# Loads of the late modulation on GpSimd's queue, with two places of their own beside three for the weights

## The chip, the cores and the metric

The kernel runs on one core of one Trainium2 chip. The metric is device microseconds of that core for one execution. Five engines matter here: TensorE (PE, with its weight loads shown as PEld), VectorE (DVE), ScalarE (ACT), GpSimd (POOL) and SyncE (SP), which does nothing but issue transfers. The times of the kernel before are those of three runs; the profile and its trace are of a further execution.

## The reference, cut to what matters

One layer of a diffusion backbone over 256 latent tokens with 256 context tokens, 2048 channels wide, all in float32. What is computed, cut to the parts that this change touches or lies beside:

```python
sh1, sc1, g1, sh2, sc2, g2 = jnp.split(jax.nn.silu(c) @ w_ada[l] + b_ada[l], 6, axis=-1)
... = split_columns(modulate(rmsnorm(x, norm_mix[l]), sh1, sc1) @ w_in[l])
# latent attention (q, k, v from low-rank projections) and gated DeltaNet, both branches
y_l = merge_branches(y_mla_l, dn_output(o_dn_l, ...), lga, lgb, w_o_mla[l], w_o_dn[l], w_out[l])
x = x + jnp.expand_dims(g1, -2) * y_l
x = x + jnp.expand_dims(g2, -2) * conv_glu(
    modulate(rmsnorm(x, norm_ffn[l]), sh2, sc2), w_ffn_up[l], ffn_conv[l], w_ffn_down[l])
```

The modulation `silu(c) @ w_ada` has six parts of 2048 numbers. The first two (`sh1`, `sc1`) are needed at once. The other four (`g1`, `sh2`, `sc2`, `g2`) are needed late: `g1` behind the output projection, `sh2` and `sc2` ahead of the feed-forward part, `g2` at the very end. These four are "the late modulation"; their weights are 64 MB, read as 128 tiles of 512 KB.

## The kernel before, in words

**Weights.** Nearly all of the time is matrix products of float32 weights with activations. A tile of weights (128 partitions x 1024 columns, 512 KB) is loaded into one of five **places** in SBUF (tag `raw`, `NR = 5`, a ring: the n-th load goes where the (n-5)-th was). ACT casts each half of it (512 columns) to `whi` (line 121), DVE subtracts to get the rest `wlo` (line 122), and PE multiplies by both parts (helper `mm_hl`; all PE instructions carry line 68). There are six places for halves of `whi` and of `wlo` (`NH = 6`). A `raw` place is free again when the `wlo` of its second half is done. `load_w` (line 130) does this for one block of columns, `raw_w` (line 124) issues the load on SP's queue (line 127).

**The late modulation.** `ada_rest` (line 254) is a generator that is run beside everything else: each step takes one of the 128 tiles of `wada2`, and one DVE instruction (line 279, shown as a custom operation) multiplies it with a row `sch` that stands on all partitions and sums it up, in place. `load(i)` (line 257) takes a place of the same ring of five (tag `raw`) and issues the load on SP's queue (line 260). It is called one step ahead: step i asks for tile i+1 and then reduces tile i. `sch` holds one half of the silu'd condition; it is loaded anew when the half changes (line 273, five times, on SP's queue).

**How it is spread.** `Side` (line 234) runs such a generator by debts: `ada(ns)` adds to what is owed, and steps of 1300 ns are taken until nothing is owed. How many steps come at which place of the program is thus fixed. They come in the DeltaNet heads (17 tiles), in the attention (`side`, line 1152 and on, 45), in the scan (line 1362, about 20), in the output projection `wout` (line 1409, 19) and in the feed-forward loop (line 1476, 27). The stages by the time at which they run: heads from 130 us, latent projections from 345, attention from 450, scan from 720, DeltaNet's output projection `wodn` from about 930, `wout` from 985, the change to the feed-forward part from 1075, its loop from 1110, its last product `wdown` from 1550 us to the end. In attention and scan, products for the gates (`gtp`, weights `wz`, `wgm`, `wgd`) and the attention's output projection (`brp`, `womla`) are put between the short, dependent products.

**What sets the order.** Engines run their own queue in order, and an instruction waits for what it reads and for its place. The program's order is not quite the queues' order: the framework plans the queues by its own costs, except for engines in stretches that are pinned (`Ordered`, line 58, keeps those in the program's order; loads by `sync.dma_start` are not pinned, those by `osync` are). On SP's queue lie the weights' loads (line 127), the late modulation's loads (line 260), the scan's small loads (lines 1225 to 1249) and others; an entry whose place is not free yet holds up all behind it. POOL has 50 instructions in the whole kernel: the power -1/2 for the norms (`rsq`, line 173) and a few fills.

**The early loads.** `load_shift` (line 329) loads the weights of `sh1` into the same ring of five.

Of the kernel before, what the change touches and what calls it, by code (L numbers as in the profile page):

```python
# [8 lines left out]
F32 = mybir.dt.float32  # L9
# [7 lines left out]
P = 128  # L17
# [9 lines left out]
G3 = 96 + 256 * N1  # L27
GR = 1024
GH = 512
NR = 5  # L30
NH = 6
AD = 0.55
GD0 = 2
# [20 lines left out]
def hybrid_block(ctx: ExitStack, tc: tile.TileContext, io, dbg=None):  # L54
    nc = tc.nc
    act, dve, pool, sync = nc.scalar, nc.vector, nc.gpsimd, nc.sync
# [23 lines left out]
    def pool_(name, bufs, side="left"):  # L80
        return tc.tile_pool(name=name, bufs=bufs, side=side, reuse_waits="tile")
# [5 lines left out]
    wr = ctx.enter_context(pool_("wr", 2))  # L87
# [31 lines left out]
    def split(raw, hi, lo):  # L119

        act.copy(hi, raw)  # L121
        dve.tensor_tensor(out=lo, in0=raw, in1=hi, op=ALU.subtract)  # L122

    def raw_w(src):
        n = src.shape[1]
        raw = wr.tile([P, GR], F32, tag="raw", name="raw", bufs=NR)[:, :n]
        sync.dma_start(raw, src)
        return raw

    def load_w(src):  # L130

        g = []
        for o in range(0, src.shape[1], GR):
            raw = raw_w(src[:, o : min(o + GR, src.shape[1])])
            for i in range(0, raw.shape[1], GH):
                n = min(GH, raw.shape[1] - i)
                hi = wp.tile([P, GH], F32R, tag="whi", name="whi", bufs=NH)[:, :n]
                lo = wp.tile([P, GH], F32R, tag="wlo", name="wlo", bufs=NH)[:, :n]
                split(raw[:, i : i + n], hi, lo)
                g.append((hi, lo))  # L140
        return lambda o, m=P: tuple(w[:, o % GH : o % GH + m] for w in g[o // GH])
# [12 lines left out]
    def mm_hl(ps, M, w, x, first, last):  # L154

        hi, lo = w
        xf = x.rearrange("p a b -> p (a b)")
        if last and not first:
            pe.matmul(ps[:M, :T], lo, x[:, 0, :], start=False, stop=False)
            pe.matmul(ps[:M, :], hi, xf, start=False, stop=True)  # L160
        else:
            pe.matmul(ps[:M, :], hi, xf, start=first, stop=False)
            pe.matmul(ps[:M, :T], lo, x[:, 0, :], start=False, stop=last)
# [90 lines left out]
    def ada_rest():  # L254


        def load(i):
            w = wr.tile([P, GR], F32, tag="raw", name="rawa", bufs=NR)
            c, n = divmod(i, 32)
            sync.dma_start(w, io["wada2"][c, (n // 16 + c) % 2, n % 16])  # L260
            return w

        parts = ad.tile([P, 2, 16], F32, name="parts")
        half, ahead = None, load(0)
        for i in range(128):
            c, n = divmod(i, 32)
            h, j = (n // 16 + c) % 2, n % 16
            if h != half:

                for _ in range(1 if i else 0):  # L270
                    yield 1300
                half, sch = h, ad.tile([P, GR], F32, tag="sch", name="sch")
                sync.dma_start(sch, Sc[h])
                for _ in range(3):
                    yield 1300
            w = ahead
            if i < 127:
                ahead = load(i + 1)
            dve.tensor_tensor_reduce(out=w, in0=w, in1=sch, scale=1.0, scalar=0.0, op0=ALU.mult, op1=ALU.add, accum_out=parts[:, h, j : j + 1])  # L279
            if n == 31:  # L280
                cs = slice(16 * c, 16 * c + 16)
                dve.tensor_tensor(out=adaT[:, cs], in0=parts[:, 0], in1=parts[:, 1], op=ALU.add)
                dve.tensor_tensor(out=adaT[:, cs], in0=adaT[:, cs], in1=bada[:, 32 + 16 * c : 48 + 16 * c], op=ALU.add)
                ada.done = c + 1
            yield 1300
# [41 lines left out]
    Sc = dram.tile([2, P, GR], F32, name="Sc")  # L327

    def load_shift(p):
        raws = []  # L330
        for m in range(4):
            raws.append(wr.tile([P, GR], F32, tag="raw", name="raw", bufs=NR))
            osync.dma_start(raws[m], io["wadab"][p, m])
        return raws

# [74 lines left out]
    def load(*what):  # L410
        for kind, n in what:
            d, f = {"w": (wts, load_scale), "s": (shifts, load_shift), "g": (grs, load_first)}[kind]
            d[n] = f(n)
# [101 lines left out]
    def gather(ps, M, out, scale=None):  # L515

        act.copy(out, ps[:M, T:])  # L517
        dve.tensor_tensor(out=out, in0=ps[:M, :T], in1=out, op=ALU.add)
# [240 lines left out]
    def head_inputs(h, side=lambda c: None):  # L759
# [12 lines left out]
        gather(ps, P, xq[:, 0])  # L772
        return xs[0], xs[1], xq

    ada = Side(ada_rest())
    ada.done = 0
    ins = {h: head_inputs(h) for h in (3, 0)}
# [191 lines left out]
    def mm3(ps, a, b, first, last):  # L969

        pe.matmul(ps, a[0], b[0], start=first, stop=False)
        pe.matmul(ps, a[0], b[1], start=False, stop=False)
        pe.matmul(ps, a[1], b[0], start=False, stop=last)
# [187 lines left out]
    for b in range(4):  # L1161
        at, pr = mla_attend(b), mla_project(b + 1) if b < 3 else iter(())
        for n in range(7):
            for st in (pr, tail, at):
                c = next(st, None)
# [289 lines left out]
    for f in range(NFF):  # L1455
# [19 lines left out]
        split(y, glu(f)[:, 0], glu(f)[:, 1])  # L1475
        ada(1000)
    ada.finish()
    for f in range(KD):
        ps = psm.tile([P, 512], F32, tag="mm", name="dps")
        W = load_w(io["wdown"][f])  # L1480
        for k in range(NFF):
            if f == KD - 1:
                mm3(ps[:, :T], W(k * P), (glu(k)[:, 0], glu(k)[:, 1]), k == 0, k == NFF - 1)
            else:
                mm_hl(ps, P, W(k * P), glu(k), k == 0, k == NFF - 1)
        yx = pf2.tile([P, T], F32, tag="fy", name="yo")
        src = ps[:, :T]
        if f < KD - 1:
            gather(ps, P, yx)
            src = yx  # L1490
        dve.scalar_tensor_tensor(out=yx, in0=src, scalar=adaT[:, 48 + f : 49 + f], in1=x1[:, f], op0=ALU.mult, op1=ALU.add)
        sync.dma_start(io["out"][f], yx)
# [103 lines left out]
```

## Time and profile before

| | |
|---|---|
| median of 3 runs | 1815.59 us (1812.57 to 1816.42) |
| the profiled execution | 1812.06 us |
| its span in the trace | 1810.3 us |
| PE busy | 1754.9 us, 97% of the span |
| DVE busy | 1366.4 us, 75% |
| ACT busy | 918.4 us, 51% |
| POOL busy | 46.1 us, 3% |
| read from HBM | 388.57 MB |

The page gives busy time by engine, a chain of waits that ended last, and groups of instructions. Other views used below: sums by stretch of time, groups of one stretch, who waited for whom, transfers with the median time from issue to landing, and the timeline. A row of groups reads: line, engine, operation, output<-inputs, shape, count, then busy time and mean duration of one in ns, then idle time of the engine just before and what ended it. In a row of stretches each engine has its busy time and number of instructions, then come PE's granted clock, the busy share of the 16 transfer engines and the rate.

### The profile page before, as it was taken

Reading aid. Unit: us, or ns where it says so; the run is one execution under the profiler, and the core shown is the slowest. Engines: PE = TensorE matmul, PEld = TensorE weight load, DVE = VectorE, ACT = ScalarE, POOL = GpSimd, SP = SyncE. Lnnn points to the kernel's source line nnn. Section 1 sums busy time; section 2 is a strip of 40 time slices with the busy share of each in tenths; the row PEclk is TensorE's granted clock in tenths of the full one; section 3 lists DMA queues with packets and bytes.
Section 4 is the critical chain, followed back from the end, with each engine's and each line's share of the span. In section 5 each row is a group of like instructions: output and inputs, shape, how many; then the busy total and the mean of one; then the engine's idle time right before and its main releaser. Section 6 shows DMA issues by size and latency. Waiting matters only on the chain.

```text
span 1810.3 us, 33551 instructions
## 1 busy us (share of the span) xinstructions
PE 1754.9 (97%) x12701; PEld 1520.6 (84%) x12701; DVE 1366.4 (75%) x2764; ACT 918.4 (51%) x1866; POOL 46.1 (3%) x50
## 2 busy tenths in 40 slices
PE   7999999999989999898999999999999999999999
PEld 6887887887878887787878888888888888888888
DVE  4787899778777787576669989888788888655554
ACT  3344444444666665433346555555555555544443
POOL 0000011000000000000010000000000000000000
PEclk9999999999999999999989999999999999999999
DMA  9973788764778767887766985777667777666663
GB/s 387 414 298 100 214 235 231 221 211 130 230 226 252 230 213 244 304 268 273 259 211 188 317 301 186 253 225 238 189 212 226 224 233 224 184 201 199 198 198 123
DMA packets 195011, 419.76 MB, mean 232 GB/s; under 512 B 61280, under 2 KB 101344, under 8 KB 192416
## 3 DMA queue, kind: packets, MB, share of 16 engines
q1 hardware_dynamic: 167664, 402.37, 68.9%
q10 hardware_dynamic: 27184, 15.23, 2.7%
q8 instruction: 100, 1.64, 0.4%
q14 instruction: 63, 0.52, 0.1%
HBM read 388.57 MB, written 28.84 MB: 231 GB/s over the span
## 4 chain that ended last, share of the span: by engine, by line
PE 75%; issue 9%; DMA 8%; DVE 6%; ACT 2%; POOL 1%; SPq 0%; POOLq 0%; ACTq 0%; DVEq 0%
PE fps L68 25%; PE dps L68 13%; PE mmp L68 11%; PE gtp L68 8%; PE fp L68 4%; DMA rawa<-in_wada 3%; PE brp L68 2%; DVE wlo L122 2%; DMA raw<-in_wadab 1%; PE amp L68 1%; PE vps L68 1%; PE op L68 1%; PE tp L68 1%; DVE rawa L279 1%; PE kps L68 1%
## 5 line engine op out<-in xcount | busy, mean ns | idle before, releaser
L122 DVE TENSOR_TENSOR wlo<-raw,whi 128x512 fp32r<-128x512 f32 (+1 forms) x940 | 632.4, 685 | 202.5 <-ACT whi L121 194.7
L121 ACT CAST whi<-raw 128x512 fp32r<-128x512 f32 (+1 forms) x940 | 573.7, 619 | 404.0 <-PE dps L68 113.7
L68 PE MATMUL fps<-H,whi 128*128 128x512 f32 x1376 | 473.9, 393 | 1.8 <-DVE H L1433 1.7
L68 PE MATMUL fps<-H,wlo 128*128 128x256 f32 x1376 | 371.6, 280 | 0.1
L68 PEld LDWEIGHTS fps<-H,whi 128*128 128x128 f32 x1376 | 253.1, 188 | 53.2 <-issue 1.9
L68 PEld LDWEIGHTS fps<-H,wlo 128*128 128x128 f32 x1376 | 259.2, 188 | 7.6 <-DVE wlo L122 0.5
L68 PE MATMUL gtp<-h,whi 128*128 128x512 f32 x640 | 232.5, 400 | 5.0 <-ACT whi L121 5.0
L68 PE MATMUL mmp<-h,whi 128*128 128x512 f32 x640 | 226.9, 397 | 0.0
L68 PE MATMUL dps<-GB,whi 128*128 128x512 f32 (+1 forms) x595 | 195.7, 378 | 0.0
L279 DVE CUSTOM_DVE_ANT_0 rawa<-rawa,sch 128x1024 f32<-128x1024 f32 x128 | 155.9, 1220 | 38.5 <-DMA rawa<-in_wada 37.7
L68 PE MATMUL gtp<-h,wlo 128*128 128x256 f32 x640 | 175.1, 284 | 5.5 <-DVE wlo L122 5.4
L68 PE MATMUL mmp<-h,wlo 128*128 128x256 f32 x640 | 176.1, 281 | 0.3 <-DVE wlo L122 0.3
L68 PE MATMUL dps<-GB,wlo 128*128 128x256 f32 x560 | 154.1, 280 | 0.0
L68 PEld LDWEIGHTS gtp<-h,whi 128*128 128x128 f32 x640 | 120.7, 190 | 30.1 <-ACT whi L121 6.6
L68 PEld LDWEIGHTS mmp<-h,whi 128*128 128x128 f32 x640 | 119.0, 188 | 24.6 <-issue 0.4
L68 PEld LDWEIGHTS gtp<-h,wlo 128*128 128x128 f32 x640 | 121.6, 190 | 13.3 <-DVE wlo L122 9.1
L68 PEld LDWEIGHTS dps<-GB,whi 128*128 128x128 f32 x595 | 109.2, 188 | 21.2
L68 PEld LDWEIGHTS mmp<-h,wlo 128*128 128x128 f32 x640 | 120.3, 188 | 3.6 <-DVE wlo L122 1.0
L68 PEld LDWEIGHTS dps<-GB,wlo 128*128 128x128 f32 x560 | 105.1, 188 | 0.6
L68 PE MATMUL fp<-h,gh 128*128 128x256 f32 (+1 forms) x448 | 85.3, 291 | 2.7 <-ACT h L68 1.7
L68 PEld LDWEIGHTS fp<-h,gh 128*128 128x128 f32 (+1 forms) x448 | 69.7, 190 | 7.6 <-issue 4.1
L517 ACT COPY fx<-fps 128x256 f32<-128x256 f32 x86 | 31.8, 372 | 65.7 <-PE fps L68 65.7
(565 smaller groups left out, 2553.4 us busy)
## 6 DMA issues: line engine op xcount, KB each, us to landing
rawa<-in_wada SPq DMA_DIRECT2D x128, 512.0 KB, 4.7
raw<-in_wgate SPq DMA_DIRECT2D x82, 512.0 KB, 4.4
raw<-in_wval SPq DMA_DIRECT2D x82, 512.0 KB, 4.5
raw<-in_wdown SPq DMA_DIRECT2D x80, 512.0 KB, 4.2
wt<-in_wadas SPq DMA_DIRECT2D x16, 1024.0 KB, 10.5
raw<-in_wadab SPq DMA_DIRECT2D x32, 512.0 KB, 8.7
raw<-in_wgm SPq DMA_DIRECT2D x32, 512.0 KB, 4.7
raw<-in_wgd SPq DMA_DIRECT2D x32, 512.0 KB, 5.4
```

The lines of the kernel that those rows point to most:

```text
L68: i = f(*a, **k)
L121: act.copy(hi, raw)
L122: dve.tensor_tensor(out=lo, in0=raw, in1=hi, op=ALU.subtract)
L279: dve.tensor_tensor_reduce(out=w, in0=w, in1=sch, scale=1.0, scalar=0.0, op0=ALU.mult, op1=ALU.add, accum_out=parts[:, h, j : j + 1])
L517: act.copy(out, ps[:M, T:])
```

## The change

The ring of five is cut in two while the late modulation runs: three places (tag `raw`) for the weights, two (tag `rawa`) for the late modulation. Its loads and the five loads of `sch` are issued on GpSimd's queue in place of SP's. Ahead of the late modulation (`load_shift`) and behind it (`wdown`), the weights use all five places in turn: `raw_tile` counts and sends two of five loads to the `rawa` places.

```diff
-NR = 5
+NR = 3
+NA = 2
...
+    place = [0, True]
+    def raw_tile():
+        place[0] += 1
+        spare = place[1] and place[0] % (NR + NA) >= NR
+        return wr.tile([P, GR], F32, tag="rawa" if spare else "raw", name="raw", bufs=NA if spare else NR)
...
     def raw_w(src):
         n = src.shape[1]
-        raw = wr.tile([P, GR], F32, tag="raw", name="raw", bufs=NR)[:, :n]
+        raw = raw_tile()[:, :n]
         sync.dma_start(raw, src)
...
         def load(i):
-            w = wr.tile([P, GR], F32, tag="raw", name="rawa", bufs=NR)
+            w = wr.tile([P, GR], F32, tag="rawa", name="rawa", bufs=NA)
             c, n = divmod(i, 32)
-            sync.dma_start(w, io["wada2"][c, (n // 16 + c) % 2, n % 16])
+            pool.dma_start(w, io["wada2"][c, (n // 16 + c) % 2, n % 16])
...
-                sync.dma_start(sch, Sc[h])
+                pool.dma_start(sch, Sc[h])
...
-            raws.append(wr.tile([P, GR], F32, tag="raw", name="raw", bufs=NR))
+            raws.append(raw_tile())
...
+    place[1] = False
     ada = Side(ada_rest())
...
     ada.finish()
+    place[1] = True
     for f in range(KD):
         ps = psm.tile([P, 512], F32, tag="mm", name="dps")
```

## Prediction

> **What bounds the kernel now.** First the page, for the share of each engine:
>
> ```profile
> span 1810.3 us, 33551 instructions
> PE 1754.9 (97%) x12701; PEld 1520.6 (84%) x12701; DVE 1366.4 (75%) x2764; ACT 918.4 (51%) x1866; POOL 46.1 (3%) x50
> ```
>
> PE is busy for 1754.9 of 1810.3 us. Whatever the change does to waits of DVE or SP, it can take from the time only what is PE's idle time now, 55.4 us, and it can add without limit. So the second view asks in which stages PE idles (sums by stretch: length, PE, PEld, DVE, ACT, POOL, clock, busy share of the transfer engines, GB/s):
>
> ```profile
> 130.00:345.00 215.00, 211.75 (x1792) 178.43 (x1791) 180.84 (x393) 103.39 (x215) 15.96 (x14) 1.00 0.68 200
> 345.00:450.00 105.00, 101.21 (x867) 84.72 (x867) 89.20 (x190) 51.57 (x106) 5.02 (x6) 1.00 0.61 176
> 450.00:720.00 270.00, 256.75 (x1911) 224.29 (x1910) 203.56 (x438) 170.59 (x388) 17.53 (x15) 0.97 0.74 231
> 720.00:900.00 180.00, 165.57 (x1361) 142.62 (x1361) 120.51 (x286) 70.36 (x141) 0.00 (x0) 0.99 0.83 279
> 900.00:985.00 85.00, 81.29 (x688) 69.64 (x683) 69.71 (x171) 42.54 (x93) 4.56 (x4) 0.94 0.59 194
> 985.00:1075.00 90.00, 90.00 (x518) 79.09 (x517) 82.53 (x163) 48.18 (x101) 0.00 (x0) 1.00 0.89 309
> 1120.00:1530.00 410.00, 410.00 (x2364) 360.39 (x2363) 335.39 (x650) 227.86 (x444) 0.00 (x0) 1.00 0.72 227
> ```
>
> PE idles 13.2 us in the attention (450 to 720) and 14.4 us in the scan (720 to 900). In the heads, the latent projections and before `wout` it idles 3.3, 3.8 and 3.7 us. In `wout` (985 to 1075) and in the feed-forward loop it never idles: there the change can only lose. The time to be won lies in two stages, 27.7 us at most.
>
> **Attention.** The third view, groups of DVE, transfers and SP's waits of that stretch (a wait's row: us in total, times, longest), then DVE's timeline round PE's longest idle time:
>
> ```profile
> L279 DVE CUSTOM_DVE_ANT_0 rawa<-rawa,sch 128x1024 f32<-128x1024 f32 x45 | 54.9, 1222 | 28.8 <-DMA rawa<-in_wada 28.1 <-DMA sch<-Sc 0.6
> ```
> ```profile
> rawa<-in_wada SPq DMA_DIRECT2D x45, 512.0 KB, 4.7
> ```
> ```profile
> SPq L260 <- DVE wlo L122: 22.0, 16, 3.0
> SPq L260 <- DVE parts L279: 20.6, 11, 4.3
> ```
> ```profile
> 515.53 0.20 DVE L1109 TENSOR_SCALAR mns<-mns,qm 128x1 f32<-128x1 f32 x1
> 518.30 1.23 DVE L279 CUSTOM_DVE_ANT_0 rawa<-rawa,sch 128x1024 f32<-128x1024 f32 x1 [2.57 <-DMA rawa<-in_wada]
> 519.46 0.08 DVE L279 DVE_READ_ACCUMULATOR2_ANT parts<- 128x1 f32 x1
> 519.46 0.16 DVE L1011 SCALAR_TENSOR_TENSOR km<-ks,krm 128x4 f32<-128x4 f32 x1
> ```
> ```profile
> 519.67 0.58 PE L68 MATMUL vps<-whi,kvn 128*128 128x256 f32 x1 [4.04 <-DVE km L1011]
> ```
>
> DVE stands still 28.1 us for tiles of the late modulation, which nobody needs before `wout`, 470 us later. Once this reaches PE: from 515.7 DVE waits for a tile, `km` stands behind it in DVE's queue, and PE idles 4.04 us for `km`. The loads come late because SP issues them late: at line 260 it waits 42.6 us in these two rows, mostly for a place.
>
> *With the change* a load waits only for the place of two steps before. 45 steps in 270 us are one in 6.0 us, so a place has 12.0 us for one turn. What POOL takes for an issue the trace doesn't show. The nearest rows are 0.33 us for SP's issue and 1.12 us for POOL's power:
>
> ```profile
> L260 SPq DMA_DIRECT2D rawa<-in_wada x128: 327/328/652, 170.0 to 1516.7; - x128
> ```
> ```profile
> L173 POOL TENSOR_TENSOR l2m<-l2m,half 128x4 f32<-128x4 f32 (+1 forms) x16 | 18.0, 1124 | 331.0 <-DVE l2m L683 331.0
> ```
>
> [...] A turn is then 1.1 + 4.7 (landing) + 1.3 (reduction with its read) = 7.1 us, under 12.0. Waits are left only where three steps come in one burst. Of the 28.1 us of DVE I expect under 12 to be left; of PE's idle time I count the 4.04 us that are plainly from this and 0.5 us more: **-4.5 us**. Bounds: -13.2 (all of the stage's idle time), +4 (bursts bring the same waits back beside another small operation).
>
> **Scan.** Groups of PE and waits of SP in 720 to 900, then SP's timeline in it:
>
> ```profile
> L68 PE MATMUL gtp<-h,whi 128*128 128x512 f32 x209 | 77.5, 406 | 5.0 <-ACT whi L121 5.0
> L68 PE MATMUL gtp<-h,wlo 128*128 128x256 f32 x210 | 58.4, 289 | 5.5 <-DVE wlo L122 5.4
> L68 PE MATMUL brp<-YM,whi 128*128 128x512 f32 x88 | 32.6, 401 | 1.9 <-ACT whi L121 1.9
> L68 PE MATMUL brp<-YM,wlo 128*128 128x256 f32 x88 | 23.0, 282 | 2.0 <-DVE wlo L122 2.0
> ```
> ```profile
> SPq L260 <- DVE wlo L122: 25.0, 8, 6.8
> SPq L260 <- DVE parts L279: 8.8, 2, 8.5
> ```
> ```profile
> 799.26 0.52 SPq L127 DMA_DIRECT2D raw<-in_wgd  x1
> 808.37 0.33 SPq L260 DMA_DIRECT2D rawa<-in_wada  x1
> 808.79 1.26 SPq L1247 DMA_DIRECT2D jit<-As  x2
> ...
> 813.01 0.33 SPq L127 DMA_DIRECT2D raw<-in_wgd  x1
> 813.84 0.33 SPq L127 DMA_DIRECT2D raw<-in_womla  x1
> ```
>
> All of the stage's idle time is PE waiting for split weights (5.0 + 5.5 + 1.9 + 2.0 = 14.4 us). Ahead of it SP stands 33.8 us in its queue at loads of the late modulation without a place, and the weights' and the scan's loads stand behind them: 8.5 us from 799.8 to 808.4 in the lines shown. On POOL's queue such a wait holds up nothing here, since POOL has no instruction in this stage (0.00 in the row of stretches). Against it stand the three places: weights that were fetched four at a time now come three at a time. 38 loads (26 `wgd`, 12 `womla`) in 180 us through three places leave 14 us for a turn, enough on the mean, not within a bunch. I count 6 of the 14.4 us, under half: **-6 us**. Bounds: -14.4 and +4 (two bunches cut by the third place, at a landing time each).
>
> **`wout`.** This is where three places are tight. Transfers, SP's waits and DVE's main row of 985 to 1075, and the page's row of the casts:
>
> ```profile
> raw<-in_wout SPq DMA_DIRECT2D x30, 512.0 KB, 5.2
> rawa<-in_wada SPq DMA_DIRECT2D x18, 512.0 KB, 5.3
> ```
> ```profile
> SPq L127 <- DVE wlo L122: 17.6, 16, 2.9
> SPq L127 <- DVE parts L279: 17.6, 12, 3.5
> ```
> ```profile
> L122 DVE TENSOR_TENSOR wlo<-raw,whi 128x512 fp32r<-128x512 f32 x66 | 44.0, 685 | 3.3 <-ACT whi L121 3.1
> ```
> ```profile
> L121 ACT CAST whi<-raw 128x512 fp32r<-128x512 f32 (+1 forms) x940 | 573.7, 619 | 404.0 <-PE dps L68 113.7
> ```
>
> About 32 tiles of weights (two small ones among them) and 18 others pass five places in 90 us: 10 turns a place, 9.0 us each, and SP waits 35.2 us for places, so they bind already. Afterwards three places make 32/3 = 10.7 turns: 8.4 us each. The least turn is landing 5.2, two casts and one `wlo` (0.62 + 0.62 + 0.69), 7.1 us; what lies between that and 9.0 is DVE's queue (82.53 of 90 us busy) and waiting. If a turn stays at 9.0 us, the stage grows by 10.7 x 0.6 = 6.4 us; if it gets under 8.4, by nothing. Half of the waits were for `parts`, that is for places held by the other kind, and these go. I take a third of the way: **+2 us**, bounds 0 and +6.4.
>
> **The rest.** In the feed-forward loop 150 tiles pass three places in 410 us, 8.2 us a turn:
>
> ```profile
> raw<-in_wval SPq DMA_DIRECT2D x75, 512.0 KB, 4.5
> ```
> ```profile
> ACT whi L121 <- PE fps L68: 85.2, 142, 1.2
> ```
>
> Landing 4.5 and the same 1.9 make 6.4 us, and the casts there wait for PE (85.2 us, 142 times): tiles land early and the six halves behind are full. So **0**, bound +4 (where a late tile's bytes come in between and ACT's stock doesn't cover it). In the stages 345 to 450 and 900 to 985 no late modulation runs, and two of five places lie idle: **+1**, bounds 0 and +4. POOL's powers (18.0 us for 16, 1124 ns each) stand behind a load's issue now and then: 128 issues of 1.1 us in some 1350 us, a tenth of the time, over 36 powers, half an issue each: 36 x 0.1 x 0.55 = 2 us, of which half is hidden by other products: **+1**, bounds 0 and +4. The wait that is added in POOL's queue is for a reduction two steps back, which stands in DVE's queue ahead of what the next power reads, so it holds up no power by itself. The `sch` loads (five) cost as the others do.
>
> **Sum**: -4.5 - 6 + 2 + 0 + 1 + 1 = -6.5 us. Against the profiled execution's own 1812.06 us (span 1810.3 and 1.8 around it) that is 1805.6. The median of the runs shown, 1815.59, is 3.5 us above it, so against the median the forecast is **1809.1 us**. A measurement of this kernel can tell about 0.2% (3.6 us) from no change.
>
> **Rivals.**
>
> *Three places are too few* (slower). In `wout` a turn stays at 9.0 us (+6.4), PE has no idle time to give there, the stages without late modulation lose their bound (+4), the feed-forward loop starts short (+2), the powers +1, and in the scan the cut bunches eat the gain (0); the attention's -4.5 is kept. +9: 1824.5 us. It decides from a turn of 8.4 us in `wout`. For it: PE at 90.00 of 90 us and the transfers at 0.89 there. Against it: the 17.6 us of waits for `parts`, which go. Chance 0.29.
>
> *The same transfers on another queue* (no change). The bytes and the 16 engines are the same, at 0.83 busy in the scan. If what PE waits for there is bytes and not SP's order, the tiles land no earlier: attention -4.5, scan 0, losses +4: 1815.1 us. Against it: 33.8 us in which SP stood with nothing to do. Chance 0.22. [...]
>
> *POOL's loads are slow* (slower). Over 12.0 - 1.3 = 10.7 us from release to landing, every step in the attention waits: DVE's 28.1 us come back and more, gains there turn into +4, the scan keeps half (-3), losses +4: 1820.6 us. Chance 0.05. [...]
>
> **How the numbers follow.** Forecast 0.44, the others 0.29, 0.22 and 0.05. What no view shows is how the framework plans the queues anew; it moves every case by some us. The likeliest case's own range is 1803 to 1812 (won 12 us to 4 us). The wide range goes from 60% of the 27.7 us won and nothing lost (1815.6 - 16.6 = 1799) to 1828, the first rival with some us more. Faster 0.44, same 0.22, slower 0.34.
>
> **What would show it.** Right: DVE's idle time for `rawa` in the attention under 12 us; PE's in the scan at 8 us or less and no long gap in SP's queue; POOL's issues near 1.1 us; `wout` still with PE near its full time. Wrong: PE idle in `wout` or in the feed-forward loop for `whi` or `wlo`; turns there over 8.4 us; `rawa` landing over 10 us; powers on POOL behind a load.

## The result, and the profile after

| | before | after |
|---|---|---|
| median | 1814.16 us (4 runs, 1812.57 to 1816.42) | 1885.4 us (4 runs, 1876.95 to 1888.6) |
| ratio | | 1.0384, 95% interval 1.0348 to 1.0421 |
| the profiled execution, its span | 1812.06, 1810.3 us | 1884.88, 1883.1 us |

The changed kernel is slower by some 70 us, far outside the range of the prediction. First the changed kernel's page, the same two lines that the prediction starts from:

```profile
span 1883.1 us, 33670 instructions
PE 1776.1 (94%) x12701; PEld 1537.9 (82%) x12701; DVE 1373.1 (73%) x2764; ACT 922.4 (49%) x1866; POOL 116.4 (6%) x183
```

PE has the same 12701 products, is busy 21.2 us longer, and idles 107.0 us where it idled 55.4. To see where, both traces are cut at the same marks: 120 us, the first product of the attention's keys, the first of the scan, the first of the scan's norm, the first of `wout`, the first of the feed-forward part, the first of `wdown`. So the rows are heads with the latent projections, attention, scan, `wodn`, `wout`, feed-forward loop. Columns as in the prediction. The kernel before:

```profile
120.00:443.00 323.00, 318.09 (x2737) 270.00 (x2735) 273.57 (x584) 154.26 (x321) 20.99 (x20) 1.00 0.66 196
443.00:747.90 304.90, 287.89 (x2097) 250.13 (x2096) 225.03 (x474) 189.30 (x423) 17.53 (x15) 0.98 0.75 236
747.90:934.70 186.80, 174.00 (x1525) 150.58 (x1526) 129.71 (x318) 69.80 (x143) 0.00 (x0) 0.99 0.80 269
934.70:993.40 58.70, 54.99 (x401) 46.19 (x401) 53.79 (x132) 33.10 (x76) 4.56 (x4) 0.91 0.54 171
993.40:1087.60 94.20, 90.64 (x565) 80.04 (x563) 84.16 (x164) 49.74 (x102) 0.70 (x1) 1.00 0.88 303
1087.60:1568.00 480.40, 480.22 (x2753) 421.43 (x2754) 393.26 (x769) 269.10 (x527) 0.00 (x0) 1.00 0.70 219
```

The changed kernel, cut at the same marks:

```profile
120.00:471.50 351.50, 329.93 (x2754) 278.98 (x2743) 301.56 (x633) 153.24 (x319) 49.42 (x73) 0.96 0.74 228
471.50:832.90 361.40, 304.10 (x2097) 262.24 (x2096) 267.76 (x563) 191.76 (x426) 58.41 (x94) 0.89 0.79 254
832.90:1000.70 167.80, 167.80 (x1523) 149.29 (x1521) 111.35 (x280) 71.31 (x142) 0.00 (x0) 1.00 0.74 229
1000.70:1057.80 57.10, 53.10 (x401) 44.73 (x401) 51.38 (x127) 31.50 (x74) 4.59 (x4) 0.97 0.55 169
1057.80:1157.30 99.50, 93.17 (x566) 81.78 (x564) 69.18 (x129) 52.98 (x106) 0.69 (x1) 0.97 0.66 196
1157.30:1640.40 483.10, 481.27 (x2752) 421.38 (x2753) 366.13 (x713) 268.76 (x527) 0.00 (x0) 1.00 0.62 187
```

The heads took 28.5 us more and the attention 56.5 us more; the scan took 19.0 us less; the rest makes some 7 us. VectorE's column tells what happened: in the attention it has 563 instructions where it had 474, in the feed-forward loop 713 where it had 769. The late modulation has moved. Its reductions, first the kernel before, then the changed one (ns: least, median, greatest; first and last start in us):

```profile
L279 DVE CUSTOM_DVE_ANT_0 rawa<-rawa,sch x128: 1205/1219/1227, 173.7 to 1521.4; 128x1024 f32<-128x1024 f32 x128
```
```profile
L288 DVE CUSTOM_DVE_ANT_0 rawa<-rawa,sch x128: 1201/1219/1277, 136.9 to 801.9; 128x1024 f32<-128x1024 f32 x128
```

All 128 are now done by 803 us: 49 in the heads (17 before) and 79 in the attention (47). Counted in VectorE's queue, the last of them stood behind 2234 of its 2508 other instructions and now stands behind 1039. The generator still takes its steps where it did; but the reductions and their loads are not pinned, and with places of their own they no longer wait for the weights' turn, and the framework's planner put them far earlier.

The price, in one place. VectorE's timeline of the changed kernel, then PE's:

```profile
494.32 1.22 DVE L288 CUSTOM_DVE_ANT_0 rawa<-rawa,sch 128x1024 f32<-128x1024 f32 x1
...
497.81 1.23 DVE L288 CUSTOM_DVE_ANT_0 rawa<-rawa,sch 128x1024 f32<-128x1024 f32 x1 [2.26 <-DMA rawa<-in_wada]
...
502.52 1.23 DVE L288 CUSTOM_DVE_ANT_0 rawa<-rawa,sch 128x1024 f32<-128x1024 f32 x1 [3.48 <-DMA rawa<-in_wada]
...
505.35 1.23 DVE L288 CUSTOM_DVE_ANT_0 rawa<-rawa,sch 128x1024 f32<-128x1024 f32 x1 [1.59 <-DMA rawa<-in_wada]
...
518.00 1.23 DVE L288 CUSTOM_DVE_ANT_0 rawa<-rawa,sch 128x1024 f32<-128x1024 f32 x1 [1.34 <-DMA rawa<-in_wada]
519.16 0.08 DVE L288 DVE_READ_ACCUMULATOR2_ANT parts<- 128x1 f32 x1
519.16 0.16 DVE L1021 SCALAR_TENSOR_TENSOR km<-ks,krm 128x4 f32<-128x4 f32 x1
```
```profile
519.46 0.60 PE L69 MATMUL ks<-ones,ksq 128*32 128x1 f32 x32 [19.99 <-DVE km L1021]
```

Eight reductions stand in a row; from 494.3 to 519.2 us VectorE does nothing else. Two places hold two loads in flight, so seven of the eight wait for a landing (0.78 to 3.48 us each), and `km` of 0.16 us, the first of the attention's eight, stands behind them all. In the kernel before it was the third `km` that held PE, for 4.04 us behind one load; now the first holds it for 19.99 us behind eight. The group of the attention's reductions, whose idle time was to fall under 12 us:

```profile
L288 DVE CUSTOM_DVE_ANT_0 rawa<-rawa,sch 128x1024 f32<-128x1024 f32 x79 | 96.4, 1221 | 50.7 <-DMA rawa<-in_wada 47.7 <-DMA sch<-Sc 2.9
```

It rose from 28.8 to 50.7 us.

### The profile page after: what moved, and what is told of

The parts are those of the page before. It is cut to its first block, busy times and chain, and to the rows that moved or that the text cites. A ratio compares the mean times of both kernels' runs of the same rounds, so it can differ in the third digit from the quotient of the medians.

```text
span 1883.1 us, 33670 instructions
## 1 busy us (share of the span) xinstructions
PE 1776.1 (94%) x12701; PEld 1537.9 (82%) x12701; DVE 1373.1 (73%) x2764; ACT 922.4 (49%) x1866; POOL 116.4 (6%) x183
## 3 DMA queue, kind: packets, MB, share of 16 engines
q0 software_dynamic: 19152, 69.74, 11.7%
## 4 chain that ended last, share of the span: by engine, by line
PE 60%; issue 22%; DMA 8%; DVE 6%; POOL 3%; ACT 1%; SPq 0%; POOLq 0%; DVEq 0%; ACTq 0%
PE fps L69 25%; PE dps L69 13%; PE mmp L69 5%; PE gtp L69 4%; DMA rawa<-in_wada 3%; PE fp L69 3%; PE brp L69 3%; POOL rawa L269 2%; DVE rawa L288 1%; DMA raw<-in_wadab 1%; DVE wlo L123 1%; PE amp L69 1%; DMA raw<-in_wz 1%; PE op L69 1%; DMA sch<-Sc 1%
## 5 line engine op out<-in xcount | busy, mean ns | idle before, releaser
L123 DVE TENSOR_TENSOR wlo<-raw,whi 128x512 fp32r<-128x512 f32 (+1 forms) x940 | 639.7, 686 | 244.7 <-ACT whi L122 230.1
L69 PE MATMUL gtp<-h,whi 128*128 128x512 f32 x640 | 237.0, 407 | 0.0
L69 PEld LDWEIGHTS dps<-GB,whi 128*128 128x128 f32 x595 | 109.3, 188 | 21.2
L269 POOL DMA_DIRECT2D rawa<-in_wada x128 | 69.3, 542 | 577.9 <-DVE parts L288 369.0
```

Of the source, the lines that this page charges most:

```text
L69: i = f(*a, **k)
L269: pool.dma_start(w, io["wada2"][c, (n // 16 + c) % 2, n % 16])
```

## The experiments

The theories at first. **T1**: the reductions come too early, because nothing holds them. **T2**: GpSimd's queue is at fault. **T3**: three places are too few for the weights. The parts were taken singly (places, queue), and the changed kernel was given an edge (an order between two instructions that the planner has to keep) that holds its reductions in the program's order.

**places_only** and **queue_only**: the diff of the change without its `pool.dma_start`, and nothing but its `pool.dma_start`.

> The changed kernel with the loads on SyncE's queue: places of their own, no new queue, no edge. T1: the planner again hoists the reductions (112 of 128 lie among VectorE's first 1034 others, the last 16 reach to the 1334th), so the time stays near the changed kernel's: 1855 to 1890 us. T2: about 1815 us. T3: 1870 to 1890 us.

> The kernel before with the loads on GpSimd's queue: the ring of five stays shared. T1: the reductions stand as before (last at 2235), so 1805 to 1830 us, whatever the new queue is worth by itself. T2: 1870 to 1890 us. T3: 1805 to 1825 us.

Measured: places_only 1.0121 (1.0090 to 1.0152), queue_only 1.0105 (1.0079 to 1.0131) times the kernel before; medians 1835.29 and 1835.13 us. Each part costs about 1%, both together 3.8%: the parts don't add, and no theory had said that. places_only hoists (moves its reductions forward) nearly as far as the changed kernel (45 reductions in the heads, 67 in attention) and loses a third as much, so T1 in its plain form fell here; it misses queue_only by 5 us too. T2 and T3 miss both kernels by 10 us or more. In queue_only the reductions stand on the mean 4 instructions from where they stood, the last one behind 2234 others as before, so its 1% is not their order.

**held** and **held_sp**: the changed kernel, and places_only, with one edge.

```diff
-            dve.tensor_tensor_reduce(out=w, ...)
+            red = dve.tensor_tensor_reduce(out=w, ...)
+            tc.keep_in_program_order(red)
```

> The changed kernel with one edge more: each of the 128 reductions may not be issued ahead of the vector instruction that the program has before it. Theory T1 (the reductions come too early: with places of their own nothing holds them, so the planner puts them all among the first 1040 of VectorE's 2510 other instructions, where before they reached to the 2235th): the last one goes back to place 2291, heads and attention fall back to about 323 and 305 us from 351.5 and 361.4, and the time lies in the range of the prediction, 1799 to 1828 us, near 1810. Theory T2 (GpSimd's queue is at fault: its loads are slow, or its powers stand behind its loads): it stays at 1870 to 1890 us. Theory T3 (three places are too few for the weights): 1870 to 1890 us as well.

> As held, but the loads of the late modulation come from SyncE's queue again. T1: 1799 to 1828 us, within some 8 us of held. T2: about 1815 us, and 55 us or more below held. T3: 1870 to 1890 us.

Measured: held 1.0091 (1.0070 to 1.0112), 1832.29 us; held_sp 1.0075 (1.0055 to 1.0096), 1829.08 us. The edge alone takes 53 us of the loss back, with GpSimd's queue and three places left as they are, so T2 and T3, which gave held 1870 us or more, fall; both times lie 1 to 4 us above the upper end that T1 gave. The rows of held for heads, attention and `wout`:

```profile
120.00:447.50 327.50, 322.56 (x2766) 273.60 (x2758) 275.96 (x586) 155.26 (x321) 30.99 (x39) 0.99 0.64 191
447.50:760.30 312.80, 288.92 (x2098) 250.72 (x2098) 223.69 (x471) 189.81 (x426) 41.94 (x62) 0.97 0.74 237
991.50:1101.60 110.10, 93.30 (x566) 80.76 (x564) 86.22 (x167) 49.63 (x103) 10.81 (x20) 0.95 0.78 266
```

Heads and attention are back within 8 us each of the kernel before; `wout` is 15.9 us longer. Between held and held_sp, with one order, the medians are 3 us apart and the intervals overlap. By stages the queue does tell: with the loads on GpSimd's queue the scan is 9.8 us shorter (173.7 for 183.5), and attention and `wout` are 4.3 and 6.0 us longer (312.8 for 308.5, 110.1 for 104.1). Their transfers (median us from issue to landing), held first:

```profile
rawa<-in_wada POOLq DMA_DIRECT2D x128, 512.0 KB, 5.3
```
```profile
rawa<-in_wada SPq DMA_DIRECT2D x128, 512.0 KB, 4.5
```

A load from GpSimd lands 0.8 us later in this pair, and 0.2 us later in the pair before_order and before_order_sp below (5.2 and 5.0).

**before_held**: the edge on the kernel before.

> The kernel before (five shared places, SyncE's queue) with the edge of held. It prices the edge by itself: if held and held_sp lost their 14 to 16 us to the edge, this one takes 1825 to 1835 us; if they lost them to the three places and the new queue, 1811 to 1818 us.

Measured: 1.0261 (1.0235 to 1.0287), 1862.19 us, above both expectations. With five shared places the program's own order is dear by itself, which was not foreseen; its row for `wout`:

```profile
1009.10:1135.40 126.30, 103.86 (x566) 84.40 (x564) 87.17 (x165) 50.13 (x102) 1.09 (x1) 0.94 0.70 225
```

At that order, places of their own are worth a good deal: held_sp, with three and two, takes 33 us less than this kernel with five shared. With this T3 is out as the cause of the 70 us.

**unburst**: the changed kernel, with an edge on the reductions 50 to 56, which breaks up the eight of above.

```diff
+            if 50 <= i < 57:
+                tc.add_manual_dep(red.ins, kms[0].ins.name, ...)
```

> The changed kernel with one edge for the reductions 50 to 56: not ahead of the first key statistic km of the attention. It breaks up the one place where the changed kernel has eight reductions in a row on VectorE, with km behind them and TensorE idle for 19.99 us; the first 50 reductions stand where they stood, and no run longer than four is left, that at the very end. Theory W (what costs is the wait: reductions that stand in a row wait for a load each, two at a time, and the small operation behind them holds TensorE): 15 to 25 us less than the changed kernel, 1860 to 1870 us. Theory D (what costs is VectorE's work alone: 128 reductions of 1.2 us in the two stages): 1878 to 1890 us.

Measured: 1.0300 (1.0264 to 1.0336), 1869.42 us: 16 us less than the changed kernel, within what W gave. The trace is less clear: the 19.99 us are gone, the attention is 8.0 us shorter (353.4 for 361.4), and PE now waits 12.7 and 7.2 us at its end for the weights of `brp`. So one burst was worth less than its own length.

**lead32**: the changed kernel, a reduction at most 32 steps ahead of its place.

```diff
+            seen.append(last_dve())
             red = ...
+            if i >= 32:
+                tc.add_manual_dep(red.ins, seen[i - 32], ...)
```

> The changed kernel where a reduction may come at most 32 steps ahead of its place in the program. Heads and latent keep the 48 or so reductions of the changed kernel, attention falls from 79 to about 44, scan to wout get some again, and 16 are left for the feed-forward part. If hoisting is the cause, the time lies between held (1832) and the changed kernel (1885): 1850 to 1865 us, with heads still at about 350 us. If it is the queue or the number of places, 1875 to 1890 us.

Measured: 1.0160 (1.0119 to 1.0200), 1842.91 us, less than expected. Heads 348.8 us with 48 reductions, as said; attention 309.4 us with 47.

**same_order**: the changed kernel, each reduction not ahead of the instruction behind which it stands in places_only.

```diff
+    BEHIND = [1929, 1929, 1697, 1669, ...]
...
+            tc.add_manual_dep(red.ins, "I-%d" % BEHIND[i], ...)
```

> The changed kernel (loads on GpSimd's queue, two places, three for the weights), with an edge for each reduction: not ahead of the vector instruction behind which it stands in places_only. VectorE's order is then nearly that of places_only, which differs from the changed kernel in the loads' queue alone and took 1835 us; no eight reductions stand in a row. If the 50 us between places_only and the changed kernel come from the order that the planner chose for the new queue (the reductions more crowded), it takes 1835 to 1850 us, with heads at 326 to 332 us. If they come from the queue itself (issue and landing of its loads, its powers), 1870 to 1885 us, with heads near 350 us.

Measured: 1.0202 (1.0165 to 1.0240), 1852.48 us, just above the range for the order and well below that for the queue. In the trace the reductions stand on the mean 3 instructions from where they stand in places_only. Of the 50 us between places_only and the changed kernel, some 33 are the order that the planner chose when the loads went to GpSimd. The other 17 are the queue at a crowded order together with what the edges and a new plan of SyncE's queue may add; no run here parts them. The heads, same_order then places_only:

```profile
120.00:456.90 336.90, 328.17 (x2789) 277.41 (x2787) 301.35 (x631) 156.69 (x325) 47.84 (x68) 0.98 0.74 231
```
```profile
120.00:446.20 326.20, 319.00 (x2737) 270.62 (x2736) 296.70 (x626) 153.84 (x321) 20.99 (x20) 1.00 0.77 241
```

**Five attempts at a better kernel, and what they say of number and crowding.** The scan is some 19 us shorter without its reductions (167.7 us in places_only), and places_only had 28 more in the heads for 3.2 us. So the steps were moved: **moved** (the kernel before, three rates changed), **fenced2** and **fenced3** (places_only, the same kind of rates, the reductions that come from `wout` on held behind a fence at its start, and behind a second one at the feed-forward part), **moved_held_sp** (held_sp with the rates of moved), **moved_part** (its edge from attention on only).

```diff
-AD = 0.55
+AD = 0.33
...
-ADS = 0.3
+ADS = 0.0
...
-ADB = 4000
+ADB = 11500
```

The further edits of the fenced kernels (AD 0.5 and 0.53, ADS 0.0, ADB 8000 and 9000) and of moved_part:

```diff
+            if fence[0]:
+                tc.add_manual_dep(red.ins, fence[0], ...)
...
+    behind()
     while ada.done < 1:
```
```diff
+            if hold[0]:
+                tc.keep_in_program_order(red)
...
+    hold[0] = True
     pe.pinned = True
     for c in mla_project(0):
```

> The kernel before with three rates changed and nothing else: 48 of the late modulation's reductions in the stage of the heads (17 before), 29 in attention (48), none in the scan (18), 18 in wout, 33 in the feed-forward part. From the runs so far heads took 28 more for 3.2 us, attention 20 more for 26 us, and the scan without its 18 was 19 us shorter. If a reduction's price is set by the stage where it stands, 1775 to 1800 us. If early reductions are dear wherever they stand, 1825 us or more.

> places_only with two fences: the reductions that the program has from wout on may not come before wout, and those of the feed-forward part not before it; none is traced in the scan. So 45 reductions in the heads, 30 in attention, none in the scan and wodn, 24 or so in wout, the rest behind. If prices by stage add up (heads 3 us over the kernel before, as in places_only; attention 20 us under it, as 18 fewer at 1.1; scan 19 us under it; wout and the feed-forward part 5 us over), 1780 to 1795 us. If early reductions in the heads cost 25 to 29 us, as in moved and lead32, 1805 to 1825 us.

> As fenced2, with rates that bring 80 reductions ahead of the scan: 47 in the heads, 33 in attention, 18 or so in wout. By the prices of the stages within 5 us of fenced2: 1780 to 1797 us; 1805 to 1825 us if the heads cost 25 us more.

> Two places of their own and three for the weights on SyncE's queue, the edge of held, and the rates of moved: 48 reductions in the heads, 29 in attention, none in the scan, 19 in wout, each at its place in the program and so evenly spread. If early reductions are cheap when they are spread and have places of their own (theory W), heads take 326 to 335 us, attention 294 to 302, the scan 168, wout 104 to 110, and the whole 1795 to 1812 us. If their number in the heads or the three places cost (moved: heads 352.4 us with the five shared), heads take 345 us or more and the whole 1820 to 1835 us.

> As moved_held_sp, but the edge only from attention on: in the heads the planner may hoist again. Theory W: hoisting in the heads costs as little as in places_only (326.2 us for 45 reductions), so heads 326 to 333 us and the whole 1793 to 1810 us, within 5 us of moved_held_sp. If the number counts, 1820 to 1835 us as well.

| kernel | reductions: heads, attention, scan, `wout`, after | heads, attention, scan, `wout`, feed-forward us | ratio, 95% interval |
|---|---|---|---|
| before | 17, 47, 18, 19, 27 | 323.0, 304.9, 186.8, 94.2, 480.4 | 1 |
| after | 49, 79, 0, 0, 0 | 351.5, 361.4, 167.8, 99.5, 483.1 | 1.0384 (1.0348 to 1.0421) |
| moved | 49, 29, 0, 19, 31 | 352.4, 294.2, 169.2, 108.8, 482.3 | 1.0070 (1.0045 to 1.0094) |
| fenced2 | 45, 30, 0, 23, 30 | 328.5, 319.7, 167.8, 107.9, 497.8 | 1.0150 (1.0121 to 1.0178) |
| fenced3 | 47, 33, 0, 23, 25 | 331.0, 316.2, 167.7, 107.5, 492.9 | 1.0144 (1.0110 to 1.0177) |
| moved_held_sp | 48, 29, 0, 19, 32 | 367.0, 303.8, 167.7, 110.4, 482.5 | 1.0244 (1.0220 to 1.0267) |
| moved_part | 48, 29, 0, 19, 32 | 346.2, 304.6, 167.7, 111.9, 483.8 | 1.0165 (1.0142 to 1.0189) |

None beats the kernel before, and all five sums by stages were wrong; moved alone came out as its other theory had it, moved_held_sp and moved_part lie above both of theirs, the fenced ones too. A reduction has no price that goes with its stage. With 45 to 49 of them the heads take from 326.2 (places_only) to 367.0 us, and the spread ones of moved_held_sp are the dearest, so "spread is cheap" fell with "early is dear". Only the scan is regular: without reductions it takes 167.7 to 169.2 us in all of them.

**before_order** and **before_order_sp**: the whole change, and its places alone, with the list of same_order filled from the kernel before. In the traces the reductions stand on the mean one instruction from where they stood.

> The whole change (GpSimd's queue, two places and three), with an edge for each reduction: not ahead of the vector instruction behind which it stands in the kernel before. So all 128 stand where they stood before, to some places. This is the premise on which the prediction was worked out. If the steps of the prediction hold under it, 1799 to 1828 us, near 1809: attention some 4 and the scan some 6 us shorter, wout 2 longer. If the new queue or the three places cost by themselves, 1830 us or more; the changed kernel's 1885 us would mean that the order has no part.

> As before_order, with the loads on SyncE's queue: the places alone, with the order of before. If the places by themselves cost nothing at the same order, 1805 to 1818 us. If the new queue costs 15 us at the same order, as between places_only and same_order, this one is 15 us under before_order; if it costs 3 us, as between held_sp and held, 3 us under it.

Measured: before_order 1.0045 (1.0025 to 1.0065), 1820.94 us; before_order_sp 1.0028 (1.0014 to 1.0042), 1818.76 us. The medians are 2 us apart, so at this order too the queue is worth little in all. This settles the main point. The change as it is costs 3.84%, the same change with the order of before 0.45%: at 1814 us, some 61 of 70 us are the order. Attention, scan and `wout` of before_order, then the group of its reductions in the attention:

```profile
441.60:758.20 316.60, 290.91 (x2097) 252.87 (x2097) 227.06 (x475) 189.82 (x424) 42.97 (x63) 0.96 0.74 234
758.20:931.70 173.50, 169.43 (x1525) 150.90 (x1526) 129.02 (x317) 69.90 (x142) 10.05 (x19) 0.99 0.84 278
989.20:1098.30 109.10, 95.02 (x565) 81.77 (x563) 86.80 (x170) 50.77 (x106) 10.84 (x20) 0.94 0.80 270
```
```profile
L290 DVE CUSTOM_DVE_ANT_0 rawa<-rawa,sch 128x1024 f32<-128x1024 f32 x47 | 57.1, 1219 | 11.0 <-DMA rawa<-in_wada 11.0
```

VectorE's waits for the late modulation fall from 28.8 to 11.0 us, and the attention is 11.7 us longer all the same. Its longest wait, PE's, ScalarE's and SyncE's timelines:

```profile
743.00 0.79 PE L69 MATMUL brp<-YM,whi 128*128 128x512 f32 x1 [8.97 <-ACT whi L122]
```
```profile
742.33 3.66 ACT L122 CAST whi<-raw 128x512 fp32r<-128x512 f32 x6 [5.43 <-DMA raw<-in_womla]
```
```profile
731.44 1.52 SPq L1248 DMA_DIRECT2D jit<-Xq  x2
735.91 0.30 SPq L1248 DMA_DIRECT2D jit<-Xo  x1
736.26 0.45 SPq L1209 DMA_DIRECT2D gt<-Gs  x1
736.80 0.41 SPq L136 DMA_DIRECT2D raw<-in_womla  x1
```

SyncE's queue was planned anew as well: a load of `womla` now stands behind the scan's small loads, is issued at 736.80 and lands after 742; the edges hold VectorE's order only. The same wait, 6.6 us long, is in before_order_sp, and there the attention takes as long as in the kernel before and the scan 5.1 us less:

```profile
442.70:747.60 304.90, 287.46 (x2097) 250.79 (x2096) 226.37 (x476) 189.34 (x424) 17.13 (x15) 0.97 0.76 240
747.60:929.30 181.70, 173.75 (x1522) 151.84 (x1521) 128.49 (x317) 69.21 (x142) 0.00 (x0) 0.98 0.82 271
```

So the 11.7 us of before_order come with the loads on GpSimd's queue, or with the plan that goes with it; the places alone don't bring them.

**late_shared**: before_order_sp, with five shared places again from `wout` on.

```diff
         def load(i):
-            w = wr.tile([P, GR], F32, tag="rawa", name="rawa", bufs=NA)
+            w = raw_tile() if place[1] else wr.tile([P, GR], F32, tag="rawa", name="rawa", bufs=NA)
...
+    place[1] = True
     while ada.done < 1:
```

> before_order_sp up to the scan, and from wout on the five places shared by weights and late modulation, as in the kernel before. If wout's 10 us over the kernel before (104.0 against 94.2) come from the places (three turns for the weights, two for the steps, at a step each 5 us), wout falls back to 94 to 97 us, the scan stays at 182, and the whole takes 1803 to 1812 us. If they come from the edges, wout stays at 102 us or more and the whole at 1815 to 1820 us.

Measured: 1.0008 (0.9993 to 1.0023), 1817.93 us, no difference that can be told from the kernel before. `wout` of before_order_sp, then of late_shared:

```profile
987.80:1091.80 104.00, 93.53 (x565) 81.78 (x563) 86.94 (x169) 51.92 (x106) 1.19 (x1) 0.95 0.82 283
```
```profile
989.80:1093.10 103.30, 92.95 (x565) 80.41 (x564) 86.53 (x170) 49.40 (x103) 0.69 (x1) 0.97 0.84 281
```

`wout` keeps its 9 us though it has its five places, so the places there are not what makes it longer. Edges aren't needed for it either: queue_only and moved have none, and five shared places, and their `wout` takes 111.0 and 108.8 us. In late_shared some 4 of the 9 us are one wait of PE at the stage's end, for a square of `x1` on ScalarE (`x1q`); the kernel before, then late_shared:

```profile
PE ss L68 <- ACT x1q L1406: 0.8, 1, 0.8
```
```profile
PE ss L69 <- ACT x1q L1420: 4.9, 1, 4.9
```

## Why the prediction was wrong

**The step that failed** is the premise of the attention's term, "45 steps in 270 us are one in 6.0 us, so a place has 12.0 us for one turn": that the steps stay where they stand. The prediction named the gap and sized it at nothing: "What no view shows is how the framework plans the queues anew; it moves every case by some us." It moved this one by some 61 us. The shared ring did two things. It made the late loads wait, which the profile shows, and it kept their reductions beside the weights of the same stretch, which no wait shows. The change removed both.

The terms, read in before_order, where the premise holds (its profiled execution took 1826.16 us, 5.2 above that kernel's median, so a stage can read long by as much):

- *Attention, -4.5*: wrong sign. The waits went as forecast (11.0 us, under 12, and PE's wait for `km` 0.7 us for 4.0); the stage grew by 11.7 us (316.6 for 304.9), 9.0 of it in one wait for a load of `womla`. With the places alone (before_order_sp) it came out at nothing, 304.9 us. The term counted what a faster late load frees, not where the weights' loads go in SyncE's new order.
- *Scan, -6*: right in kind, and the forecast is under half of what came: -13.3 us (173.5 for 186.8), near the bound of -14.4. PE's idle time fell from 12.8 to 4.1 us, and the rest is PE's busy time, 4.6 us less. That SyncE's queue was freed is borne out: with one order and the same places, the scan is 8.2 us shorter with the loads on GpSimd's queue than on SyncE's (before_order, before_order_sp), 9.8 us in held and held_sp, and 10.7 us in queue_only and the kernel before.
- *`wout`, +2*: +14.9 us (109.1 for 94.2), beyond the bound of 6.4. The turns of three places aren't what the term missed, as late_shared shows; with the loads on SyncE's queue it is +9.8 (104.0).
- *Feed-forward loop, 0*: +2.9 us, within the bound of 4.
- *Stages without late modulation, +1*: nothing seen; heads with the latent projections -1.4, `wodn` -1.2 us.
- *GpSimd's issue at 1.1 us*: no run shows this value, the author's estimate beside the 1.12 us of a power; the issue took 0.53 us, half of it. Its row in the changed kernel:

```profile
L269 POOL DMA_DIRECT2D rawa<-in_wada x128: 527/528/711, 106.2 to 793.9; - x128
```

- *GpSimd's powers, +1*: 13 of the 36 in the changed kernel start behind a load, by 0.8 us at most; between VectorE's result and the power lie 14.7 us in all for 11.4 before. Within the bound.

Of the rivals, "three places are too few" had the sign and the wrong mechanism: the feed-forward loop lost 2.7 us, and at the program's order the places gained 33. "POOL's loads are slow" fell by the 5.1 us median landing in the changed kernel. "The same transfers on another queue" comes nearest for the whole time at the order of before (1.0045 and 1.0028, intervals that overlap); the totals of that pair and of held and held_sp are 2 and 3 us apart. By stages the rival fails: it gave the scan nothing, and the scan gained 8 to 11 us by the queue, while attention (4 to 12 us) and `wout` (5 to 17 us) lost it again in the same three pairs. With five shared places queue_only lost 19 us by it, and same_order lies 17 us above places_only; the rival counts neither.

Still open: by what the planner came to crowd the reductions more when their loads went to GpSimd (its reckoning isn't in a trace); what in an order sets its price, since neither number nor spread does; why the loads on GpSimd's queue make attention and `wout` longer; and what is left of the 9 to 15 us of `wout` at the order of before.

## What to carry to other kernels

A shared ring of buffers is also an order: whoever gives a side job its own buffers, in a program whose queues a planner fills, frees the job from its place, and must either pin it there or look at the new queues before reckoning any wait. Work that nobody needs for long should be anchored to the instruction beside which it is cheap, by an edge of order alone; here such edges brought 1885 back to 1821 us with the change left as it is. Before pricing a stage by its number of side steps, move some and measure: five sums of that kind failed here.

## What was not expected of the hardware

Idle time of PE cost more than its length here. Stretches of the changed kernel from the end of the 19.99 us on (the column before the last two is PE's granted clock):

```profile
519.00:522.00 3.00, 2.54 (x41) 2.56 (x42) 1.76 (x6) 0.00 (x0) 1.56 (x2) 0.50 0.71 202
522.00:525.00 3.00, 3.00 (x12) 2.68 (x11) 2.77 (x8) 0.37 (x1) 1.32 (x2) 0.50 0.53 143
525.00:528.00 3.00, 3.00 (x16) 2.59 (x14) 2.30 (x6) 1.24 (x2) 1.26 (x2) 0.81 0.32 128
528.00:531.00 3.00, 3.00 (x26) 2.95 (x25) 2.10 (x5) 1.74 (x5) 0.53 (x1) 1.00 0.74 198
```

PE comes back at half clock (0.50 in the first two rows) and has its full clock, 1.00, within 9 us (519.5 to 528). Over the attention the granted clock is 0.89 for 0.98, and the same 2097 products are busy 304.1 us for 287.9: 16.2 us of the stage's 56.5 are no idle time at all. The prediction's terms and rivals counted idle time only. The clock was not at its full value before the 19.99 us either: it is 0.50 in the 3.5 us of products ahead of them (496.0 to 499.5), which follow a wait of PE of 4.67 us. In rows of 1 us it is 0.50 up to 526, 0.92 in the next and 1.00 from 527 on, which makes some 6.7 us of work at half clock from 519.5 on (an estimate that takes the 0.92 for a mix of 0.50 and 1.00). What sets that length, no run here shows.
